# Order-only ties for the first chunk's gather, two places for the samples' states, expert rows from one queue, and an earlier fence slot

## Chip, cores and metric

The kernel runs on one core of a Trainium2 chip. The metric is the device time of one execution, in microseconds. The engines of the core are named as in the profile: PE (TensorE, matrix products; PEld is its weight load), DVE (VectorE), ACT (ScalarE), POOL (GpSimd) and SP (SyncE, which only issues transfers). Every engine works through its own list of instructions in the order in which they were placed at build time. ACT and SP issue plain transfers, each into a DMA queue of its own; POOL issues the indirect ones. All of them share 16 DMA engines.

## What is computed

One step of a decoder layer for 512 prompt tokens and 32 sample tokens (8 sequences of 4), model width 1024, all in float32:

```python
proj = x @ w_in + b_in                      # q, k, v, g, ca, cg: 512 columns each
q, k = rope(q), rope(k) * 128 ** -0.5
o, state = retention(q, k, v, state0)       # 4 heads, chunks of 128 tokens
ret  = silu(g) * head_norm(o)
conv = silu(layer_norm(depthwise31(ca * sigmoid(cg))))
x = layer_norm(ALPHA * x + concat(ret, conv) @ w_out)
# PEER: 8 heads, 128 x 128 product keys, the 16 best experts per head
idx, gate = topk(x @ w_query, sub_keys_1, sub_keys_2)     # 128 experts per token
act = gelu(u[idx] . x)
x = layer_norm(ALPHA * x + sum(gate * act * v[idx]))
```

There are 16384 experts, each with a row u and a row v of 1024 numbers. Besides the two y there go out the new retention states (one for the prompt, one for each sample sequence) and the new convolution caches.

## The kernel before, in words

The 544 tokens are laid out as the first prompt chunk (128 tokens), then the 32 samples, then the three other chunks. Two ways are used for the experts:

- **Gather.** For the first chunk, the samples and the second chunk, `gather` (L568 to L587) works slot by slot. A slot is one indirect transfer on POOL (L573) that fetches, for 128 (token, expert) pairs, u and v side by side, 8 KB each, into one buffer. DVE then takes the dot product of u with the token (L576, the "dot"), ACT applies gelu and the gate (L580, L581), and DVE adds v times the weight to the sum (L586, the "acc"). The first chunk has 128 slots, the samples 32 (four experts of each token at a time) and the second chunk 128. Four buffers go round for most of this (three in `gp`, one more in `gx` or `gx2`; three for the first chunk's slots from `KX` = 60 on).
- **Dense.** For the last 256 tokens, `scores_of` (L781) computes u of all 128 x 128 experts against the tokens on PE. A "key" is 128 experts: one row of 512 KB from the table `ut` (issued on L784), eight products on L787 (16 records in the profile), then gelu on ACT (L833, L838, or L886 and L888 in `s_stage`). The gates are put into a dense table by one-hot products (`build`, L858: ACT on L865 and L867, DVE on L869 and L873, PE on L878), and `first_keys` (L891) multiplies them into the scores (L902) or copies them (L904). Then `phases` runs over the rows of v, again 512 KB each (issued on L919), with products on L925 (8 records a row).

Rows of `ut` and `uv` go through four buffers (`UV`, L35), and `turns` (L774) issues them alternately from SP and from ACT.

The time runs in these stages. The first chunk goes through the whole layer up to its top-k first; then its gather slots are spread over the work on the other tokens: the samples' states (`retain_s`, L385), the convolution (L255) and its norm (`conv_norm`, L285), the retention of the three other chunks (`retain`, L704, with `head_norm`, L318), and the output projection with the layer norms (`mix_a` and `mix_b`, L723 to L738; `layer_norm`, L442; its transposes for the next product are on L487). Then come the query projection, the top-k of the other tokens (`retrieve`, L511) and, on PE, the scores of the first 76 keys. Then the build of `first_keys`, within which the scores of 20 more keys are made (`s_stage`). Its last product is the **fence**: the samples' slots from `FREE` = 24 on (L37, used on L577) and all slots of the second chunk have their dots behind it. Behind the fence `phases` (PE) and `fetched` (the rest of the gather, with `finish` and its stores on L596) run side by side. At the very end the last 256 tokens get their layer norm from PE's sums, and are stored.

`retain_s` goes over the eight sample sequences in pairs. Each round takes one tile from `keys_or_scratch` (a single buffer): its first half holds the states of two sequences (`r0`, loaded from ACT's queue on L404), the other half two copies of v, each masked to one sequence (`vx`, L403). PE uses the states (L408) and makes the update (L412, 256 columns), DVE adds it, and SP stores the new states (L415).

What orders the work: the tile framework simulates a timeline at build time, takes instructions in the order in which they can start there, and so fixes each engine's list. `behind(ins, other)` (L166) adds a tie that only says "not before this one in the list"; no semaphore is added by it. The fence is such a tie.

## Time and profile before

| quantity | value |
|---|---|
| median of 3 runs | 1601.7 us (1597.08 to 1602.1) |
| the profiled execution's own time | 1610.35 us |
| its span | 1608.6 us |
| mean granted clock of PE in it | 0.968 |
| DMA traffic | 503.75 MB, mean 313 GB/s |

The same page cuts the span into 40 slices of 40.2 us. A digit is the busy share of a slice in tenths; PEclk is the granted clock of PE, and 9 is 90% or more:

```profile
PE   6899989996879997999999997989999999999997
DVE  3939989989774999999866989667777677776642
ACT  2225352244221323333623799512994111111100
PEclk9999989997989999999999997999999999999999
DMA  9458678997789768998699721989999999999972
```

PE is the engine with the fullest row. The slices that are not full on PE lie at the start, at 200 us, at 360 to 480 us (the norms of the convolution and of the output projection), at 600 to 640, at 965 to 1005 us (the end of the build) and at 1045 to 1085 us. DVE follows the gather. ACT has its peak in the two builds (880 to 1000 us and around 1160 us). The DMA engines are nearly idle in the second half of the build and full from about 1085 us to 1530 us.

In the views quoted further down, a row of the waits tells which engine's operation waited, what for, the total in us, how often and the longest. A row of a timeline tells start and duration in us, engine, line, operation, output and inputs, and in square brackets the idle time before it with what ended it. A group of lines tells busy time, mean duration in ns of one, and the idle time before it.

### The profile page before, as it was taken

The numbers are of one execution on the slowest core, as the hardware profiler recorded it, in microseconds if no ns is written. First come the engines' busy times: TensorE is split into PE (matmuls) and PEld (weight loads), VectorE is DVE, ScalarE is ACT, GpSimd is POOL, SyncE is SP. The second block draws the span as 40 slices with busy tenths as digits, with TensorE's granted clock in tenths as the row PEclk, the third lists the DMA queues.
The fourth block names the chain that finished last, engine by engine and source line by source line (L and its number), as shares of the span: only waits on it lengthen the run. The fifth ranks groups of instructions, "written<-read, shape, count | busy, mean of one in ns | idle before, by whom it ended". The sixth has DMA issues, their size and how long they took to land.

```text
span 1608.6 us, 20726 instructions
## 1 busy us (share of the span) xinstructions
PE 1481.2 (92%) x7014; PEld 1016.0 (63%) x7014; DVE 1223.1 (76%) x3158; ACT 601.6 (37%) x1687; POOL 394.4 (25%) x335
## 2 busy tenths in 40 slices
PE   6899989996879997999999997989999999999997
PEld 6788557554666666888888885434566655644443
DVE  3939989989774999999866989667777677776642
ACT  2225352244221323333623799512994111111100
POOL 1001323433431222221122100233223223333200
PEclk9999989997989999999999997999999999999999
DMA  9458678997789768998699721989999999999972
GB/s 356 178 200 350 247 252 294 345 356 253 262 338 360 254 232 311 351 333 313 221 390 375 282 80 58 374 344 417 375 350 387 418 406 420 416 423 424 425 263 94
DMA packets 99542, 503.75 MB, mean 313 GB/s; under 512 B 10183, under 2 KB 21191, under 8 KB 56549
## 3 DMA queue, kind: packets, MB, share of 16 engines
q0 software_dynamic: 42240, 305.12, 48.9%
q1 hardware_dynamic: 32317, 122.84, 20.5%
q10 hardware_dynamic: 24880, 74.47, 12.4%
q8 instruction: 55, 0.90, 0.2%
q14 instruction: 50, 0.41, 0.1%
HBM read 497.03 MB, written 5.80 MB: 313 GB/s over the span
## 4 chain that ended last, share of the span: by engine, by line
PE 32%; DMA 28%; DVE 20%; issue 12%; POOL 5%; ACT 2%; ACTq 0%; POOLq 0%; SPq 0%; DVEq 0%
DMA g<-in_uv_dram,Ib 15%; PE pB L925 12%; PE sp L787 9%; DMA g<-in_uv_dram,I 8%; DVE acc L586 5%; PE mm L199 5%; POOL g L573 4%; DVE g L576 3%; PE mm L878 2%; DMA uv<-in_uv_dram 2%; DMA g<-in_w_in_dram 2%; DVE score L506 1%; PE mm L309 1%; PE mm L476 1%; DVE iu L505 1%
## 5 line engine op out<-in xcount | busy, mean ns | idle before, releaser
L787 PE MATMUL sp<-x1T,uv 128*128 128x256 f32 x2048 | 465.9, 383 | 25.4 <-DMA uv<-in_ut_dram 13.1
L787 PEld LDWEIGHTS sp<-x1T,uv 128*128 128x128 f32 x2048 | 386.0, 191 | 99.1 <-issue 27.7
L586 DVE SCALAR_TENSOR_TENSOR acc<-g,wgt,acc 128x1024 f32<-128x1024 f32 x285 | 364.8, 1280 | 102.1 <-ACT wgt L581 101.3
L573 POOL DMA_INDIRECT g<-in_uv_dram,I x128 | 177.1, 1384 | 451.9 <-DVE acc L586 253.5
L580 ACT ACTIVATE act<-act 128x1 f32<-128x1 f32 x288 | 57.8, 201 | 611.5 <-DVE g L576 599.9
L573 POOL DMA_INDIRECT g<-in_uv_dram,Ib x128 | 158.2, 1236 | 431.7 <-DVE acc L586 238.0
L576 DVE SCALAR_TENSOR_TENSOR g<-g,x1g 128x1024 f32<-128x1024 f32 x160 | 195.6, 1224 | 89.1 <-DMA g<-in_uv_dram,Ib 60.5
L576 DVE SCALAR_TENSOR_TENSOR g<-g,x 128x1024 f32<-128x1024 f32 x128 | 155.4, 1215 | 38.2 <-DMA g<-in_uv_dram,I 38.0
L199 PE MATMUL mm<-x1T,w 128*128 128x384 f32 (+1 forms) x512 | 177.6, 503 | 0.0
L925 PE MATMUL pB<-uv,Ga 128*128 128x512 f32 x352 | 157.2, 594 | 4.5 <-DMA uv<-in_uv_dram 4.4
L865 ACT ACTIVATE off<-row,e1T 128x128 bf16<-128x128 bf16 x512 | 157.7, 388 | 1.6 <-PE sp L787 0.6
L199 PEld LDWEIGHTS mm<-x1T,w 128*128 128x128 f32 x512 | 97.5, 192 | 71.9 <-issue 39.5
L925 PE MATMUL pB<-uv,Gb 128*128 128x512 f32 x256 | 117.4, 613 | 6.1 <-DMA uv<-in_uv_dram 5.6
L925 PEld LDWEIGHTS pB<-uv,Ga 128*128 128x128 f32 x352 | 66.3, 190 | 77.2 <-issue 67.4
L925 PE MATMUL pB<-uv,Gd 128*128 128x512 f32 x256 | 111.0, 593 | 2.9 <-DMA uv<-in_uv_dram 2.9
L925 PEld LDWEIGHTS pB<-uv,Gd 128*128 128x128 f32 x256 | 48.3, 190 | 65.4 <-issue 60.5
L925 PEld LDWEIGHTS pB<-uv,Gb 128*128 128x128 f32 x256 | 48.7, 196 | 64.2 <-issue 55.3
L878 PEld LDWEIGHTS <-A 128*128 128x128 bf16 x1536 | 64.4, 99 | 35.3 <-issue 26.3
L878 PE MATMUL mm<-B,A 128*128 128x96 bf16 (+1 forms) x1536 | 67.8, 196 | 11.6 <-DVE Gc L904 10.0
L873 DVE TENSOR_TENSOR B<-M,gtT 128x768 bf16<-128x768 bf16 (+1 forms) x192 | 69.5, 418 | 11.6 <-PE mm L878 11.6
L925 PE MATMUL pB<-uv,Gc 128*128 128x512 f32 x160 | 73.0, 601 | 0.0
L867 ACT ACTIVATE A<-off 128x1024 bf16<-128x1024 bf16 x64 | 67.4, 1053 | 14.4 <-PE mm L878 10.3
(279 smaller groups left out, 1701.5 us busy)
## 6 DMA issues: line engine op xcount, KB each, us to landing
uv<-in_ut_dram ACTq DMA_DIRECT2D x80, 512.0 KB
uv<-in_uv_dram SPq DMA_DIRECT2D x80, 512.0 KB
uv<-in_ut_dram SPq DMA_DIRECT2D x48, 512.0 KB
uv<-in_uv_dram ACTq DMA_DIRECT2D x48, 512.0 KB
w<-in_w_in_dram SPq DMA_DIRECT2D x18, 1024.0 KB
w<-in_w_query_dram SPq DMA_DIRECT2D x16, 1024.0 KB
w<-in_w_out_dram SPq DMA_DIRECT2D x7, 1024.0 KB
g<-in_uv_dram,I POOLq DMA_INDIRECT x128, 8.0
```

The source lines that it names most:

```text
L199: T.matmul(p[:, :n], w[m // 2][:, k, (m % 2) * 128:(m % 2 + 1) * 128], xT[:, k, c0:c0 + n], start=(k == 0), stop=(k == 7))
L309: mm = T.matmul(p[:n, q * 256:(q + 1) * 256], xT[:, k, c0:c0 + n], w[q][:, k, :], start=(k == 0), stop=(k == 7))
L573: G.indirect_dma_start(out=t, out_offset=None, in_=a["uv"], in_offset=bass.IndirectOffsetOnAxis(ap=idx[:, k:k + 1], axis=0))
L576: dot = V.scalar_tensor_tensor(t[:, :D], t[:, :D], 1.0, x1, op0=OP.mult, op1=OP.mult, accum_out=act[:, 0:1])
L580: S.activation(act[:, 1:2], act[:, 0:1], AF.Gelu)
L586: V.scalar_tensor_tensor(acc, v, wgt, acc, op0=OP.mult, op1=OP.add)
L787: T.matmul(sp, u[:, k], x1T[:, k, NG2:], start=(k == 0), stop=(k == 7))
L865: S.activation(off[:, t], row, AF.Abs, bias=e1T[:, t1 + t:t1 + t + 1])
L867: S.activation(A, off, AF.Relu, bias=1.0, scale=-1.0)
L873: V.tensor_tensor(B[:, q], M, pairs_of(gtT[:, q], t1).to_broadcast([128, TB // 2, ne, 2]), op=OP.mult)
L878: T.matmul(pt[:, t % nt], A[:, t - t1], B[:, q, (t - t1) // 2, :, t % 2], start=(q == 0), stop=(q == 2))
L925: T.matmul(pB[b][q], W[:, b * 128:(b + 1) * 128], vt[:, q * 512:(q + 1) * 512], start=False, stop=(e == NK - 1), skip_group_check=True)
```

## The change

Four things are changed.

1. `hold(k, ins)` notes that the first chunk's dots from slot k on stand behind `ins` on DVE. There are seven such notes: slot 48 behind the last small step of the second chunk's head norm, 50 behind the last multiplication of `conv_norm`, 52 behind the same head-norm step of the last chunk, and 56, 60, 64 and 68 behind the last addition of the four layer norms of `mix_b`.
2. `retain_s` takes one tile for all rounds. Its two halves hold the states of one pair and of the next in turn; the masked copies of v are two small tiles, and the update is two products of 128 columns in place of one of 256.
3. All rows of `ut` and `uv` are issued from SP. `turns` is gone.
4. `FREE` is 12 and no longer 24: the samples' slots from 12 on stand behind the fence.

```diff
--- before.py
+++ after.py
@@ -1,5 +1,4 @@
 from contextlib import ExitStack
-from itertools import cycle
 
 import numpy as np
 import concourse.bass as bass
@@ -34,7 +33,7 @@
 TB = 8
 KX = 60
 UV = 4
-FREE = 24
+FREE = 12
 EG = (32, 20, 44, 32)
 E0S = (0, 32, 52, 96)
 
@@ -297,10 +296,11 @@
         S.activation(rs[:, :n], pv[:, :n], AF.Sqrt, bias=eps_c)
         V.reciprocal(rs[:, :n], rs[:, :n])
         for m in range(4):
-            V.tensor_mul(y[:, m, :n], y[:, m, :n], rs[:, :n])
+            last = V.tensor_mul(y[:, m, :n], y[:, m, :n], rs[:, :n])
             S.activation(y[:, m, :n], y[:, m, :n], AF.Silu, bias=cg_b[:, m:m + 1], scale=cg_g[:, m:m + 1])
-
-    bv = [None]
+        return last
+
+    bv, steps = [None], {}
 
     def project_v(w, xT, c0, n, v=None, after=None):
         p = mmps()
@@ -327,7 +327,7 @@
         rsqrt(rs[:n], rs[:n])
         V.tensor_mul(rs[:n], rs[:n], cc("gq_" + kind)[:n])
         nb = small("hnb", [128, H])
-        V.scalar_tensor_tensor(nb[:n], mv[:n, :, 0], -1.0, rs[:n], op0=OP.mult, op1=OP.mult)
+        steps[kind] = V.scalar_tensor_tensor(nb[:n], mv[:n, :, 0], -1.0, rs[:n], op0=OP.mult, op1=OP.mult)
         on = small("on", [128, 512])
         for h in range(H):
             S.activation(on[:n, h * DH:(h + 1) * DH], po[:n, h * DH:(h + 1) * DH], AF.Identity,
@@ -395,12 +395,12 @@
         for h in range(H):
             T.matmul(po[:, h * n:(h + 1) * n], v[:n, h * DH:(h + 1) * DH], sc[:n, h * n:(h + 1) * n],
                      start=(h == 0), stop=False, skip_group_check=True)
+        room = keys_or_scratch()
         for b in range(0, SB, 2):
-            room = keys_or_scratch()
-            r0 = room[:, 0:D].rearrange("p (b h e) -> p b h e", b=2, h=H)
-            vx = room[:n, D:].rearrange("p (b e) -> p b e", b=2)
+            r0 = room[:, b // 2 % 2 * D:(b // 2 % 2 + 1) * D].rearrange("p (b h e) -> p b h e", b=2, h=H)
+            vx = [small("on", [128, 512]) for _ in range(2)]
             for j in range(2):
-                S.activation(vx[:, j], v[:n], AF.Copy, scale=cc("blk")[:n, b + j:b + j + 1])
+                S.activation(vx[j][:n], v[:n], AF.Copy, scale=cc("blk")[:n, b + j:b + j + 1])
             nc.scalar.dma_start(r0, a["state_retention"][0, b:b + 2].rearrange("b h d e -> d b h e"))
             for h in range(H):
                 for j in range(2):
@@ -409,7 +409,9 @@
                              start=False, stop=(h == H - 1 and b + j == SB - 1), skip_group_check=True)
             for h in range(H):
                 pk = mmps()[:, 0:256]
-                T.matmul(pk, kt[:n, h * DH:(h + 1) * DH], vx[:, :, h * DH:(h + 1) * DH], start=True, stop=True)
+                for j in range(2):
+                    T.matmul(pk[:, j * DH:(j + 1) * DH], kt[:n, h * DH:(h + 1) * DH], vx[j][:n, h * DH:(h + 1) * DH],
+                             start=True, stop=True)
                 V.scalar_tensor_tensor(r0[:, :, h], r0[:, :, h], float(GAMMA[h] ** SQ),
                                        pk.rearrange("p (b e) -> p b e", b=2), op0=OP.mult, op1=OP.add)
             nc.sync.dma_start(o[4][0, b:b + 2].rearrange("b h d e -> d b h e"), r0)
@@ -453,7 +455,7 @@
         for q, c in enumerate(halves if src else [slice(0, D)]):
             S.activation(t[:n, c], src[q][:n] if src else t[:n, c], AF.Identity, bias=rs[:n, 1:2], scale=rs[:n, 0:1])
             V.tensor_mul(t[:n, c], t[:n, c], g[:n, c])
-            V.tensor_add(t[:n, c], t[:n, c], b[:n, c])
+            steps["ln"] = V.tensor_add(t[:n, c], t[:n, c], b[:n, c])
 
     bv[0] = bc_row("b_v", a["b_in"][:, 1024:1536], 512, fe)
 
@@ -563,7 +565,11 @@
         V.reciprocal(sm[:n], sm[:n])
         V.tensor_mul(gate[:n, e0:e0 + nh], ex[:n], sm[:n].unsqueeze(2).to_broadcast([n, nh, TK]))
 
-    gx2, fence = [], []
+    gx2, fence, held = [], [], {}
+
+    def hold(k, ins):
+
+        held[k] = ins
 
     def gather(x1, idx, gate, acc, slots):
 
@@ -574,6 +580,10 @@
                                  in_offset=bass.IndirectOffsetOnAxis(ap=idx[:, k:k + 1], axis=0))
             act = gw.tile([128, 2], F32, name="act")
             dot = V.scalar_tensor_tensor(t[:, :D], t[:, :D], 1.0, x1, op0=OP.mult, op1=OP.mult, accum_out=act[:, 0:1])
+            if x1 is x1_0:
+                for k0, ins in held.items():
+                    if k >= k0:
+                        behind(dot, ins)
             if fence and (len(slots) == 128 or k >= FREE):
                 behind(dot, fence[0])
             wgt = gw.tile([128, 1], F32, name="wgt")
@@ -711,11 +721,12 @@
 
     retain(1)
     retain(2)
+    hold(48, steps["p"])
     banks[:] = [ps]
     silu_gate(wg, xT, n - NS, [(0, n - NS, gT[:, :, r])], False)
     wo = load_w(a["w_out"], 0) + load_w(a["w_out"], 512)
     S.activation(y[:, :, s_], yS, AF.Copy)
-    conv_norm(y, n)
+    hold(50, conv_norm(y, n))
     S.activation(gT[:, :, s_], gS, AF.Copy)
     banks[:] = [ps, ps, ps0, ps, ps0, ps, ps, ps0]
     xrs, pms, room = {}, {}, keys_or_scratch()
@@ -740,15 +751,20 @@
     gate_heads(ons[1], C, gT, NS)
     gate_heads(ons[2], C, gT, NS + C)
     retain(3)
+    hold(52, steps["p"])
     gate_heads(ons[3], C, gT, NS + 2 * C)
     mix_a(0, NS, None)
     mix_a(NS, C, 0)
     mix_b(0, NS)
+    hold(56, steps["ln"])
     mix_a(NS + C, C, 1)
     mix_b(NS, C)
+    hold(60, steps["ln"])
     mix_a(NS + 2 * C, C, None)
     mix_b(NS + C, C)
+    hold(64, steps["ln"])
     mix_b(NS + 2 * C, C)
+    hold(68, steps["ln"])
     caches()
     gather0 = gather(x1_0, I0, g0_gates, acc0, range(PH * TK))
     for _ in range(KX):
@@ -771,8 +787,6 @@
     ln2 = [bc_row("lng", a["ln2_g"], D), bc_row("lnb", a["ln2_b"], D)]
     GW = {2: gap.tile([128, EG[2], ND], F32, name="Ga")}
 
-    turns = cycle((nc.sync, nc.scalar))
-
     def place(e):
 
         g = max(i for i in range(4) if E0S[i] <= e)
@@ -781,7 +795,7 @@
     def scores_of(e):
 
         u = uvp.tile([128, D], F32, name="uv").rearrange("p (k e) -> p k e", k=8)
-        next(turns).dma_start(u, a["ut"][e])
+        nc.sync.dma_start(u, a["ut"][e])
         sp = pdn.tile([128, ND], F32, name="sp")
         for k in range(8):
             T.matmul(sp, u[:, k], x1T[:, k, NG2:], start=(k == 0), stop=(k == 7))
@@ -916,7 +930,7 @@
 
     def v_row(e):
         vt = uvp.tile([128, D], F32, name="uv")
-        next(turns).dma_start(vt, a["uv"][e * NK:(e + 1) * NK, D:])
+        nc.sync.dma_start(vt, a["uv"][e * NK:(e + 1) * NK, D:])
         return vt
 
     def v_products(e, vt, b):
```

## Prediction, made before the changed kernel had run

> **What bounds the kernel now.** I read the first part of the page, then the waits of TensorE, then the stretches in which those waits fall.
>
> ```profile
> span 1608.6 us, 20726 instructions
> PE 1481.2 (92%) x7014; PEld 1016.0 (63%) x7014; DVE 1223.1 (76%) x3158; ACT 601.6 (37%) x1687; POOL 394.4 (25%) x335
> ```
>
> ```profile
> PE mm L340 <- ACT on L333: 13.3, 2, 11.8
> PE sp L787 <- DMA uv<-in_ut_dram: 13.1, 12, 2.3
> PE pB L925 <- DMA uv<-in_uv_dram: 12.8, 10, 4.0
> ...
> PE mm L487 <- DVE xr L456: 10.5, 1, 10.5
> PE mm L878 <- DVE Gc L904: 10.0, 8, 2.2
> ...
> PE mm L487 <- DVE lrs L452: 5.9, 1, 5.9
> PE mm L408 <- DMA keys<-in_state_retention_dram: 4.9, 1, 4.9
> PE mm L412 <- ACT keys L403: 4.0, 1, 4.0
> ```
>
> TensorE is busy for 1481.2 of 1608.6 us, so 127.4 us are all that can be won without less matmul work or a better clock. The second view gives each wait as total, times and longest. The change aims at four groups of these lines: the sample states (4.9 + 4.0), the norms of mixing stage and convolution (11.8 + 5.9 + 10.5 = 28.2), the one-hot build (10.0), and the expert rows (13.1 + 12.8 = 25.9). Together that is 73 us. Three stretches show what else is busy there; the columns are sum of time, then PE, PEld, DVE, ACT and POOL busy, the granted clock, the DMA share and GB/s:
>
> ```profile
> 376.00:476.00 100.00, 74.03 (x369) 59.85 (x370) 79.32 (x126) 28.07 (x77) 39.64 (x32) 0.86 0.76 278
> 871.00:999.00 128.00, 116.60 (x1078) 100.16 (x1077) 117.16 (x404) 110.64 (x315) 8.25 (x8) 0.93 0.44 157
> 1284.00:1528.00 244.00, 228.72 (x675) 126.77 (x676) 170.57 (x216) 37.47 (x149) 75.07 (x66) 1.00 1.01 418
> ```
>
> In the mixing stage PE idles 26 of 100 us although nothing is full: a chain of short steps limits it. In the build three engines are at 86 to 92%. In the last one the DMA engines are full (418 GB/s) and PE loses 15.3 us. So there are three limits, and one edit for each.
>
> **Part 1, the sample states (L398 to L415).** Before, one tile holds two samples' states and the scaled copies of v, so the next load waits for the store of the last.
>
> ```profile
> 189.26 0.40 SPq L415 DMA_DIRECT2D out_dram<-keys  x1
> ```
> ```profile
> 200.75 0.38 ACTq L404 DMA_DIRECT2D keys<-in_state_retention_dram  x1
> ```
>
> The load at 200.75 came 11.5 us after the store was issued, and PE waited 4.0 us for the copies (L412 <- L403) and 4.9 for the states (L408): 8.9 us. After, the first two loads start together and the copies stand in tiles of their own, so both named waits should go. But the third load still needs the half that the first store reads, and it stands in PE's order with little between, so one such wait may come back later. The split product (two of 128 columns for one of 256) streams the same 256 columns in two instructions, and I take nothing for it. Bounds: 0 (the wait only moves to the third load) and −8.9. I take **−3**, nearer to 0, because the four loads are one after the other in the same stage and only one pair is taken apart.
>
> **Part 2, dots held behind norm steps.** VectorE's order is written at build time. Gather slots of the first chunk stand among the norms:
>
> ```profile
> L586 DVE SCALAR_TENSOR_TENSOR acc<-g,wgt,acc 128x1024 f32<-128x1024 f32 x24 | 30.6, 1277 | 2.0 <-ACT wgt L581 1.6
> L576 DVE SCALAR_TENSOR_TENSOR g<-g,x 128x1024 f32<-128x1024 f32 x23 | 27.9, 1218 | 13.3 <-DMA g<-in_uv_dram,I 13.3
> ```
> (VectorE, 376 to 476, grouped by line.) They take 58.5 of its 79.3 busy us, and in front of the dots it also idles 13.3 us for gather data, with norm steps queued behind the waiting dot. PE's gaps are the consequence; here is the last one, with its neighbours on VectorE:
>
> ```profile
> 475.02 1.09 PE L487 MATMUL mm<-cst,xr 128*128 128x128 f32 x4 [10.47 <-DVE xr L456]
> ```
> ```profile
> 467.72 0.16 DVE L452 SCALAR_TENSOR_TENSOR lrs<-lmv,lrs 128x1 f32<-128x1 f32 x1 [1.31 <-POOL lrs L185]
> 471.83 1.22 DVE L576 SCALAR_TENSOR_TENSOR g<-g,x 128x1024 f32<-128x1024 f32 x1 [3.95 <-DMA g<-in_uv_dram,I]
> ...
> 474.79 1.28 DVE L586 SCALAR_TENSOR_TENSOR acc<-g,wgt,acc 128x1024 f32<-128x1024 f32 x1
> ```
>
> In the last norm alone (from L452 to its last add), the wait of 3.95, the dot of 1.22 and the sum of 1.28 stand among its steps: 6.5 us. In the changed order, slots 68 on come after that norm (in the old order dots up to slot 73 stood ahead of its end), slots 56 to 67 after the three norms before it, and slots 48 and 50 after the two steps of the second chunk and of the convolution. That is five slots less ahead of the chain's end, 5 x (1.28 + 1.22) = 12.5 us, and the wait for data falls behind the norm. The chain is not VectorE alone (ScalarE, GpSimd and PE have steps in it), so not all of it comes off. I take **−11** for the instant at which L487 of the last chunk starts (475 to about 464). Bounds: −28.2 (the three waits gone) and +4 (there are four slot buffers: a dot held back holds back the transfers behind it on GpSimd's queue, and if the data then come late in front of a later dot, a wait like the 3.95 is added).
>
> The five slots are done later, and someone has to pay: the top-k of the other chunks shares VectorE with them:
>
> ```profile
> 640.00:800.00 160.00, 151.63 (x753) 131.28 (x754) 156.39 (x616) 65.93 (x160) 34.36 (x27) 0.99 0.84 305
> ```
>
> In the changed order the number of slots between the top-k's start and its first use by PE is unchanged, and the five extra ones come behind it, ahead of the end of top-k. PE has score keys to run there (L787), so I cost it at 0; if that cover fails it is 12.5 us of VectorE.
>
> **Part 3, the fence at slot 12.** The samples' slots 12 to 23 were done ahead of the fence (the build's last product into the table), and now stand behind it. Of these, the build held (VectorE, 871 to 999):
>
> ```profile
> L576 DVE SCALAR_TENSOR_TENSOR g<-g,x1g 128x1024 f32<-128x1024 f32 x8 | 9.7, 1218 | 0.0
> L586 DVE SCALAR_TENSOR_TENSOR acc<-g,wgt,acc 128x1024 f32<-128x1024 f32 x7 | 9.0, 1279 | 0.6 <-ACT wgt L581 0.6
> ```
> 18.7 of 117.2 us leave VectorE. But ScalarE is at 110.6 and PE at 116.6 of the 128, so VectorE at 98.5 stops being the bound and PE with its clock of 0.93 becomes it: 128 − 117 = **−11**. Bounds: −18.7 (the whole load) and −5 (half of the 10.0 us of waits L878 <- L904, which stand where all three are full).
>
> With −3, −11 and −11 the fence comes 25 us earlier:
>
> ```profile
> 998.67 0.23 DVE L902 TENSOR_TENSOR Gc<-Gc,mm 128x80 f32<-128x80 f32 x1
> ```
> ```profile
> L586 DVE SCALAR_TENSOR_TENSOR acc<-g,wgt,acc 128x1024 f32<-128x1024 f32 x128 | 164.4, 1284 | 68.4 <-ACT wgt L581 68.3
> ```
> ```profile
> 1545.54 1.29 DVE L593 SCALAR_TENSOR_TENSOR yt<-x1g,acc 128x512 f32<-128x512 f32 x2
> ...
> 1552.01 1.22 DVE L456 TENSOR_TENSOR yt<-yt,lnb 128x1024 f32<-128x1024 f32 x1
> 1594.22 0.70 DVE L448 BATCH_NORM_STATS2 lst<-pB 128x6 f32<-128x512 f32 x1 [40.99 <-PE pB L925]
> ...
> 1602.09 1.29 DVE L456 TENSOR_TENSOR g<-g,lnb 128x512 f32<-128x512 f32 x2
> ```
> ```profile
> 1531.29 65.47 PE L925 MATMUL pB<-uv,Gd 128*128 128x512 f32 x152 [0.86 <-DMA uv<-in_uv_dram]
> ```
>
> Behind the fence stood 8 + 128 slots and took 998.9 to 1545.5, 4.02 us each; now it is 148. From 974 that is 595 us, so the last sum ends at 1569 instead of 1545.5, its norm at 1577. PE's last product moves from 1596.8 to 1572. The 41 us in which VectorE waited are used up: both ends now meet, and the two final norms share VectorE (5.4 us of steps in the gather's one). I add **+4** (0 to +12).
>
> **Part 4, rows from one queue.**
>
> ```profile
> q0 software_dynamic: 42240, 305.12, 48.9%
> q1 hardware_dynamic: 32317, 122.84, 20.5%
> q10 hardware_dynamic: 24880, 74.47, 12.4%
> ```
> ```profile
> uv<-in_ut_dram ACTq DMA_DIRECT2D x80, 512.0 KB
> ...
> uv<-in_uv_dram ACTq DMA_DIRECT2D x48, 512.0 KB
> ```
> ```profile
> ACT act L580 <- DVE g L576: 599.9, 216, 7.9
> ```
> ```profile
> 1057.02 0.34 SPq L596 DMA_DIRECT2D out_dram<-yt  x1
> ```
> ```profile
> 1081.33 2.93 PE L925 MATMUL pB<-uv,Gb 128*128 128x512 f32 x3 [3.96 <-DMA uv<-in_uv_dram]
> ```
>
> 128 issues leave ScalarE, which stands waiting for dots for 599.9 us and issues late whatever is behind them. All 256 now leave SyncE, which has only stores to wait for; the samples' store at 1057.0 now comes after more rows, so the PE gap of 3.96 behind it should go or shrink. On the other side stands bandwidth. q0 moved 7.2 KB a packet, q1 3.8. In full stretches a row of 512 KB is needed about every 3.5 us (8 of the 152 products in 65.47 us: 3.45), which is 150 GB/s of 418. Nothing here shows one row queue alone for long beside a full gather. Bounds: −15.3 (all that PE lost from 1284 to 1528) and +18 (that loss, 6.3%, on all 598 us from fence to PE's last product is 37.5 us, of which 15.3 + 4.0 are lost already). I take **0**, as the rows that wait are mostly those that ScalarE issued late.
>
> The Trainium skill, page "DMA: Bandwidth & Descriptors", section "Queues, rings and completion order", says that each DMA engine goes round the queues that have work, packet by packet. By that rule one row queue gets one packet of two beside the gather where two got two of three; with the packets above that is 3.8 of 11.0 KB, 144 GB/s of 418 or 3.64 us a row, an estimate, 0.19 us over 3.45: +33 us on the 172 rows that the 595 us hold, if the gather never pauses, against the 0 taken above. No row of this trace tests it, since it never shows the two side by side for long.
>
> **Rivals.** (a) *The gather behind the fence becomes the end: slower.* Place: slots 12 to 31 of the samples and the 128 of the last chunk. Price: 12 x 4.02 = 48 us against 25 of fence and the slack of 41. With its norm and store (7.7 + 5.2 us) it ends at 974 + 148 s + 13. That is 1608.6 at s = 4.20 us a slot, 4% over today's; it is slower from there on. With s = 4.2 and a fence only 15 us earlier it ends at 1619, a time of 1612. For it: the DMA engines are full already, so 12 MB more have no free place. Against: PE's rows end with it, and when one lags the other's share is free. (b) *Row starvation.* The single row queue beside the full gather costs PE the 18 us of part 4's upper bound: −21 + 18, a time of 1599. For it: packets of 3.8 against 7.2 KB. Against: 15.3 us are lost already with two queues, half of them fed by an engine that issues late. The Trainium skill's rule quoted in part 4 is this mechanism. (c) *The holds give nothing.* The five slots come back under the top-k, where VectorE is busy for 156.4 of 160 us and has no place for 12.5 us more; if PE's score keys wait for it there, only states and build are won: −3 − 11 + 4 = −10, a time of 1592. For it: that row. Against: PE idles only 8.4 us there, with keys of its own to run. (d) *The change doesn't do what it says* in part 1: the third load waits as the second did. 3 us, inside the range.
>
> **How the numbers follow.** −3 − 11 − 11 + 0 + 4 = −21 on the profiled execution's span of 1608.6 gives 1587.6. The profiled execution's own time is 1610.35 us, 1.75 around its span and 8.65 above the median of the runs, 1601.7; the 21 come off that median: **1581** (1580.7). Chances: the forecast with (d) 0.52, (c) 0.14, (b) 0.16, (a) 0.18. Low end: part 2 at two thirds of its lower bound (18.8), the build likewise (12.5), the states at 3, the rows at 4, nothing at the tail: −38, so 1563. High end: beyond (b) and into the milder half of (a), 1606. About 0.3% (5 us) is what a measurement of this kernel can tell from no change: faster takes the forecast, (c) and 0.07 of (b), 0.73; the rest of (b) and 0.01 of (a) are 0.10; slower is 0.17.
>
> **What would show it.** Part 1: the two waits at L412 and L408 shorter, no 11 us between store and next load. Part 2: L340's 11.8 and L487's 10.5 down to a few us, L487's last start near 464, and no dot between L452 and L456 of that norm. Part 3: last L902 near 974, VectorE in the build below 100 us; the last sum near 1569 and the 41 us wait before the last norm gone. Part 4: PE's waits for rows at or under 26 us, and no wait near L596's store. I am wrong if the last L902 comes later than 990, if a slot behind the fence takes over 4.2 us, or if waits for rows exceed 45 us.

## The result, and the profile after

The changed kernel takes 1594.3 us (median of 20 runs, 1585.6 to 1603.8), the kernel before 1600.0 us (20 runs, 1594.8 to 1605.4, the three of above among them). The ratio is 0.9966, with a 95% interval of 0.9952 to 0.9981: by this ratio 5.4 us faster, where 21 were forecast. The profiled execution of the changed kernel took 1598.1 us. That is 12.2 us less than the profiled execution of before, which lies 10 us above its own median, so the two traces differ by more than the kernels do.

First part of its page, and its queues:

```profile
span 1595.8 us, 20861 instructions
PE 1499.0 (94%) x7046; PEld 1015.8 (64%) x7046; DVE 1225.1 (77%) x3158; ACT 602.9 (38%) x1686; POOL 365.0 (23%) x335
...
q1 hardware_dynamic: 50749, 189.96, 31.5%
q10 hardware_dynamic: 6448, 7.36, 1.5%
```

TensorE's waits (lines are those of the changed file: L487 is now L489, L476 is L478, L878 is L892, L787 is L801, L925 is L939):

```profile
PE mm L489 <- DVE xr L458: 13.1, 1, 13.1
PE mm L892 <- DVE Gc L918: 10.0, 8, 2.2
...
PE mm L478 <- ACT blk L300: 6.0, 1, 6.0
...
PE mm L408 <- DMA keys<-in_state_retention_dram: 3.2, 1, 3.2
PE pB L939 <- DMA uv<-in_uv_dram: 2.9, 4, 1.4
...
PE mm L340 <- ACT on L333: 1.6, 1, 1.6
...
PE sp L801 <- DMA uv<-in_ut_dram: 0.2, 1, 0.2
```

Most of the named waits shrank: 11.8 us at L340 are 1.6, the 5.9 in front of L487 are gone, 8.9 us for the states are 3.2, and 25.9 us for rows are 3.1. But the last norm's wait grew from 10.5 to 13.1, the build's 10.0 did not move, and 6.0 us appeared in front of the output projection (L478; e2, e4 and e6 have them too). Nor are the waits for rows gone. PE's own list leaves out its weight load, which waits for rows as well, before and after:

```profile
PEld pB L925 <- DMA uv<-in_uv_dram: 16.5, 10, 4.8
```
```profile
PEld pB L939 <- DMA uv<-in_uv_dram: 25.1, 46, 1.5
```

Few long waits have become many short ones. PE is also "busy" for 18 us more with almost the same products, and 10.6 of these stand in the products with rows of v (449.4 us before, 460.0 after). A record of such a product is 592 ns long, while the next one can start after 431 ns (152 in 65.47 us, before), so a pause of up to 0.16 us leaves no idle time in the records. The experiments show whose mark this is: e8, with one row queue, has 460.8 us in these products, and e2 and e13, with two, have 450.0 and 449.0.

This is the pace behind the fence, over the last 32 rows of v (256 records, 8 a row), before and after:

```profile
L925 PE MATMUL pB<-uv,Gd x256: 592/592/667, 1482.9 to 1596.2; 128*128 128x512 f32 x128
```
```profile
L939 PE MATMUL pB<-uv,Gd x256: 592/592/668, 1460.8 to 1579.4; 128*128 128x512 f32 x128
```

That is 3.54 us a row before and 3.71 after. The kernel before had the later half of these rows for itself, since its gather had ended at 1545: there a row took 3.43 us, and beside the gather 3.68. After, the gather runs to the end, and 3.7 us is also the step of its last slots (32 accs from 1460.2 to 1576.0). In the stretch from 1284 to 1528 the DMA engines move 424 GB/s, where it was 418:

```profile
376.00:476.00 100.00, 81.00 (x401) 62.51 (x400) 76.68 (x118) 30.91 (x80) 32.74 (x30) 0.90 0.70 267
1284.00:1528.00 244.00, 240.82 (x655) 118.62 (x654) 170.60 (x215) 38.98 (x148) 60.96 (x65) 1.00 1.02 424
```

### The profile page after: what moved, and what is told of

It reads as the page before. It is cut to its first block, busy times and chain, and to the rows that moved or that the text cites. A ratio compares the mean times of both kernels' runs of the same rounds, so it can differ in the third digit from the quotient of the medians.

```text
span 1595.8 us, 20861 instructions
## 1 busy us (share of the span) xinstructions
PE 1499.0 (94%) x7046; PEld 1015.8 (64%) x7046; DVE 1225.1 (77%) x3158; ACT 602.9 (38%) x1686; POOL 365.0 (23%) x335
## 4 chain that ended last, share of the span: by engine, by line
DMA 29%; PE 28%; DVE 24%; issue 9%; ACT 7%; POOL 3%; SPq 0%; DVEq 0%; POOLq 0%; ACTq 0%
DMA g<-in_uv_dram,Ib 18%; PE sp L801 9%; DMA g<-in_uv_dram,I 7%; DVE acc L596 6%; PE pB L939 5%; PE mm L198 4%; DVE g L582 4%; ACT off L879 3%; POOL g L579 2%; PE mm L478 2%; PE mm L263 2%; DMA g<-in_w_in_dram 2%; PE mm L892 2%; ACT A L881 1%; PE mm L309 1%
## 5 line engine op out<-in xcount | busy, mean ns | idle before, releaser
L801 PE MATMUL sp<-x1T,uv 128*128 128x256 f32 x2048 | 465.0, 384 | 14.2 <-ACT Ga L847 7.1
L596 DVE SCALAR_TENSOR_TENSOR acc<-g,wgt,acc 128x1024 f32<-128x1024 f32 x285 | 364.8, 1280 | 116.6 <-ACT wgt L591 113.8
L801 PEld LDWEIGHTS sp<-x1T,uv 128*128 128x128 f32 x2048 | 385.9, 192 | 87.4 <-issue 14.9
L579 POOL DMA_INDIRECT g<-in_uv_dram,I x128 | 164.9, 1288 | 468.0 <-DVE acc L596 236.0
L579 POOL DMA_INDIRECT g<-in_uv_dram,Ib x128 | 135.9, 1062 | 498.0 <-DVE acc L596 314.8
L939 PE MATMUL pB<-uv,Ga 128*128 128x512 f32 x352 | 162.1, 603 | 0.6 <-DMA uv<-in_uv_dram 0.4
L939 PE MATMUL pB<-uv,Gd 128*128 128x512 f32 x256 | 117.2, 601 | 2.1 <-DMA uv<-in_uv_dram 1.0
L939 PE MATMUL pB<-uv,Gb 128*128 128x512 f32 x256 | 115.4, 604 | 2.0 <-DMA uv<-in_uv_dram 1.4
L939 PEld LDWEIGHTS pB<-uv,Ga 128*128 128x128 f32 x352 | 63.7, 189 | 82.9 <-issue 63.1
L939 PEld LDWEIGHTS pB<-uv,Gd 128*128 128x128 f32 x256 | 46.1, 189 | 73.3 <-issue 71.5
L892 PEld LDWEIGHTS <-A 128*128 128x128 bf16 x1536 | 64.0, 99 | 34.7 <-issue 26.0
L939 PEld LDWEIGHTS pB<-uv,Gb 128*128 128x128 f32 x256 | 47.6, 192 | 58.8 <-issue 52.6
L892 PE MATMUL mm<-B,A 128*128 128x96 bf16 (+1 forms) x1536 | 67.7, 195 | 11.2 <-DVE Gc L918 10.0
L939 PE MATMUL pB<-uv,Gc 128*128 128x512 f32 x160 | 72.3, 599 | 0.0
```

The costliest lines, as they stand in the source:

```text
L579: G.indirect_dma_start(out=t, out_offset=None, in_=a["uv"], in_offset=bass.IndirectOffsetOnAxis(ap=idx[:, k:k + 1], axis=0))
L596: V.scalar_tensor_tensor(acc, v, wgt, acc, op0=OP.mult, op1=OP.add)
L801: T.matmul(sp, u[:, k], x1T[:, k, NG2:], start=(k == 0), stop=(k == 7))
L892: T.matmul(pt[:, t % nt], A[:, t - t1], B[:, q, (t - t1) // 2, :, t % 2], start=(q == 0), stop=(q == 2))
L939: T.matmul(pB[b][q], W[:, b * 128:(b + 1) * 128], vt[:, q * 512:(q + 1) * 512], start=False, stop=(e == NK - 1), skip_group_check=True)
```

## The experiments

Each kernel was timed beside the kernel before. The table has all of them, with three readings of the profiled execution: the start of the last norm's transposes (L487 or its like), the build (from the first to the last table product Gb), and the time from the fence to PE's last product. "Ties" are the seven order-only notes; a number there is the slot of the last one.

| kernel | states | ties | row queues | fence slot | last norm done | build | fence to PE's end | ratio to before (95%) |
|---|---|---|---|---|---|---|---|---|
| before | old | none | 2 | 24 | 475.0 | 127.8 | 598 | 1 |
| after | new | 68 | 1 | 12 | 466.9 | 127.9 | 594 | 0.9966 (0.9952 to 0.9981) |
| e1 | new | 68 | 1 | 24 | 465.3 | 133.9 | 597 | 1.0010 (0.9985 to 1.0035) |
| e2 | new | 68 | 2 | 12 | 467.7 | 126.1 | 595 | 1.0014 (0.9987 to 1.0041) |
| e3 | new | none | 1 | 12 | 481.5 | 126.0 | 592 | 1.0042 (1.0018 to 1.0066) |
| e4 | old | 68 | 1 | 12 | 457.2 | 126.0 | 594 | 0.9885 (0.9852 to 0.9918) |
| e5 | new | none | 2 | 24 | 475.4 | 126.1 | 598 | 1.0068 (1.0037 to 1.0099) |
| e6 | new | 66 | 1 | 12 | 463.4 | 126.0 | 592 | 0.9948 (0.9920 to 0.9975) |
| e7 | old | 68 | 1 | 20 | 456.2 | 126.5 | 597 | 0.9895 (0.9859 to 0.9932) |
| e8 | old | none | 1 | 24 | 461.5 | 126.0 | 600 | 0.9992 (0.9968 to 1.0015) |
| e9 | new, issue tied | 68 | 1 | 12 | 460.6 | 127.7 | 594 | 0.9916 (0.9889 to 0.9944) |
| e10 | old | 66 | 1 | 12 | 448.8 | 126.4 | 596 | 0.9868 (0.9841 to 0.9896) |
| e11 | old | 68 | 1 | 24 | 459.1 | 136.6 | 599 | 0.9973 (0.9951 to 0.9995) |
| e12 | old | 68 | 2 | 24 | 453.4 | 134.0 | 602 | 0.9984 (0.9960 to 1.0007) |
| e13 | old | none | 2 | 12 | 467.4 | 126.0 | 595 | 1.0022 (1.0001 to 1.0043) |
| e14 | new, issue tied | 66 | 1 | 12 | 450.3 | 126.0 | 594 | 0.9902 (0.9877 to 0.9927) |

One reading comes first. Up to their last norm, before, e8 and e13 have the same instructions in the same order on every engine (the first rows of `ut` apart, which e8 issues from the other queue), and that norm is done at 475.0, 461.5 and 467.4. So a single execution scatters by 13.5 us in this stage, and the one on which the prediction rests is the latest of the three (its time, 1610.4, stands 10 us above the median). The means over kernels with the same order up to that point are what can be compared: 468.0 (old states, no ties: before, e8, e13), 456.5 (old states, ties to 68: e4, e7, e11, e12), 478.5 (new states, no ties: e3, e5), 466.6 (new states, ties to 68: after, e1, e2). By them **the ties are worth 11.5 to 11.9 us, and the new states cost 10.1 to 10.5 us** at this place. Each mean has two to four executions, and the first one carries the whole scatter of 13.5, so the differences that use it are good to some 4 us. The timed runs, which don't rest on one execution, agree on the states: e5 is 0.7% (11 us) slower than before, and e4 0.8% (13 us) faster than the changed kernel.

The builds of 127.7 to 127.9 us (before, after, e9) differ from those of 126.0 in one thing that the profile shows: the mean granted clock from 50 to 60 us into the build is 0.83 there, and 1.00 in the others. Ten microseconds at 0.83 are 1.7 us of full clock.

**e1, the fence back at 24.** `-FREE = 12` `+FREE = 24`

> The changed kernel with the fence back at slot 24. Theory 1 (the build is not limited by VectorE: TensorE is full in its first two thirds, where the dots stood; behind the fence the DMA engines are the limit, a gather slot and a row going side by side at 3.70 us each): the build stays at 128 us although slots 12 to 23 stand in it again, the last acc comes 12 x 3.7 = 44 us earlier (about 1533), the last rows run at 3.45 us, PE's last product comes 5 to 7 us earlier and the tail shrinks from 15.8 to 12 us: about 10 us faster than the changed kernel, ratio to before 0.990. Theory 2 (the prediction: the build is limited by VectorE's 18.7 us of slots): build 139 us, tail 12: about 7 us slower than the changed kernel, ratio 1.001.

The build took 133.9 us, not 128, and the kernel is 0.4% slower than the changed one: theory 1 fell in its first half. Theory 2 has the ratio (1.001), but its build of 139 did not come either. The second half of theory 1 held: the last acc came at 1533.2, 44.1 us earlier, and the tail behind PE's end shrank from 15.8 to 11.7 us.

**e2, rows from two queues again.**

```diff
-        nc.sync.dma_start(u, a["ut"][e])
+        next(turns).dma_start(u, a["ut"][e])
```

> The changed kernel with rows issued alternately from SyncE and ScalarE again. Theory 1 (the sum of the bytes behind the fence is the limit, the queues only share it out): the row pace rises or falls against the slot pace, and the end moves by less than 4 us: ratio 0.994 to 0.999. Theory 2 (a single row queue gets one turn of two beside the gather and starves PE): rows faster than 3.70 us, slots slower than 3.75, PE's last product earlier by over 5 us. Theory 3 (rows issued late by ScalarE are the loss): PE's listed waits for rows back above 20 us, ratio above 1.000.

0.5% (8 us) slower than the changed kernel, and the trace shows only part of it: fence at 986.7 against 985.7, PE's end at 1581.9 against 1580.0, a tail of 18.4 us against 15.8. The longer tail is shared by e13, the other kernel with two queues and the fence at 12: in both the last acc comes 0.2 us or less before PE's end and the tail is 18.4; with one queue and this fence it comes 2.3 to 3.7 us before, and the tail is 14.9 to 16.0. The rows did not become faster with the second queue. The last 32 again take 3.7 us each:

```profile
L942 PE MATMUL pB<-uv,Gd x256: 592/592/668, 1464.2 to 1581.3; 128*128 128x512 f32 x128
```

So theory 2 fell. Theory 1 is right about the pace, but its ratio (up to 0.999) was missed. Theory 3 has only the ratio for it: PE's listed waits for rows are 17.7 us, under its 20.

**e3, no ties; e4, the old states.** For e3 `hold` notes nothing (`-held[k] = ins` `+return`); for e4 the loop of `retain_s` is that of before.

> The changed kernel without the seven ties of the first chunk's dots. Theory 1 (the ties are worth what the traces show between 362 and the start of L489 of the last chunk, 9 us, and it survives to the end): that start about 476 in place of 467, fence 994, ratio 0.9966 + 0.0056 = 1.002. Rival: what the ties win is given back under the top-k or behind the fence, where the DMA engines set the pace: ratio 0.996 to 0.998.

> The changed kernel with the samples' states in one place as before. Prediction: 3 us slower than the changed kernel, ratio 0.9985, with the waits of L412 and L408 at 4 and 5 us again. Rival (from the traces, 0.5 us between 150 and 360): the wait is only moved to other lines; same as the changed kernel within 2 us, ratio 0.995 to 0.998.

The ties held what was forecast of them: without them the last norm is done at 481.5 and the kernel is 0.8% slower. The states did the opposite: with the old ones it is 0.8% *faster*, although the waits at L412 and L408 are back (3.2 and 5.2 us). Neither theory on e4 had that.

**e5, the states alone; e6, the last tie at slot 66.** e5 is the kernel before with the new loop in `retain_s`; e6 is the changed kernel with `-hold(68, steps["ln"])` `+hold(66, steps["ln"])`.

> The kernel before with the edit of the samples' states alone. Theory S1 (two places remove the waits at L412 and L408 and cost nothing else): 0 to 4 us faster, ratio 0.9975 to 1.000. Theory S2 (the edit moves the gather's slots against the norms behind it, which costs more than the waits; in the changed kernel it was 11 us): 5 us or more slower, ratio 1.003 to 1.008, with the start of L487 of the last chunk later than 478 us. Theory S3 (the loss is a coincidence of this edit with the ties): 0.998 to 1.002 here, no loss without the ties.

> The changed kernel with the last tie at slot 66 in place of 68. In the changed kernel the dot of slot 66 waits 5.9 us for its data in front of the last layer norm's first step, and the dot of slot 67 stands behind its reciprocal. Theory H1 (a dot that waits for data ahead of a norm step holds up the norm; what is bound must be the dots whose data come late): the last start of L489 about 6 us earlier (461 in place of 467) and the whole 4 to 6 us faster than the changed kernel, ratio 0.993. Theory H2 (the order of the chain is set by PE, ScalarE and GpSimd): same as the changed kernel, 0.9966, within 2 us.

e5 bears out S2: 0.7% slower by this edit alone. Its last norm is done at 475.4, not later than 478 as S2 had it, but 7 us behind the mean of the kernels with the old order. For e6, these are VectorE's rows of the changed kernel around its last norm, for which PE had its sums ready at 453:

```profile
458.32 1.23 DVE L582 SCALAR_TENSOR_TENSOR g<-g,x 128x1024 f32<-128x1024 f32 x1 [5.93 <-DMA g<-in_uv_dram,I]
459.47 0.08 DVE L582 DVE_READ_ACCUMULATOR g<-g,x 128x1 f32 x1
459.47 0.69 DVE L450 BATCH_NORM_STATS2 lst<-mm 128x6 f32<-128x512 f32 x1
```

The dot of slot 66 stands ahead of the norm's first step (L450) and waits 5.93 us for data. In e6 it stands behind, and PE's wait there is 4.3 us in place of 13.1:

```profile
463.35 0.88 PE L489 MATMUL mm<-cst,xr 128*128 128x128 f32 x3 [4.29 <-DVE xr L458]
```

The mechanism H1 is shown, but the norm is done only 3 us earlier (463.4 against a mean of 466.6), and 3 us, inside the intervals, is all that the whole kernel gains (0.9948 against 0.9966): from there to the build it took 398 us against 391. With the old states (e10) the same tie won 8 us at the last norm, and 4 of them were left at the build.

**e7, old states and the fence at 20; e8, one queue alone.** e7 is e4 with `FREE = 20`; e8 is the kernel before with all rows from SyncE.

> The changed kernel with the samples' states as before (e4) and the fence at slot 20 in place of 12. Theory F1 (TensorE is full for the first 40 us of the build, so eight slots more fit there at no cost, and leave the stretch behind the fence): build 126 us as in e4, last acc 8 x 3.7 = 30 us earlier (about 1536), PE's last product 2 to 5 us earlier, tail 12 in place of 15: 5 to 8 us faster than e4, ratio 0.984 to 0.986. Theory F2 (every slot in the build costs VectorE time that is missed later in it): build 130 us or more, ratio 0.989 or above.

> The kernel before with the row queue edit alone: all rows from SyncE. Theory Q1 (prediction: nothing): ratio 0.998 to 1.002. Theory Q2 (from e2: the single queue saves 7 us, by ScalarE's late issues): 0.995 to 0.997, PE's listed waits for rows under 8 us. Theory Q3 (one turn of two beside the gather starves PE): rows at 3.70 us while the gather runs, 1.002 or above.

In e7 the build stays at 126.5 us with six dots in it, as F1 had it, and the last acc comes 30 us earlier, but the kernel is not faster than e4 (0.9895, where F1 had 0.984 to 0.986): from fence to PE's end it takes 597 us in place of 594. In all kernels with the fence at 20 or 24 this stretch takes 597 to 602, and with the fence at 12, which puts more slots behind it, 592 to 596; no run shows why. e8 changes nothing in the time that can be measured, as the prediction had it, although PE's listed waits for rows fall from 25.9 us to 3.5.

**e9, one issue tied behind a root.** What do the new states change 120 us later? These are the rows of the changed kernel around the convolution's norm, first GpSimd and then VectorE. The root of the head norm (L183, L184) and the gather's issues (L579) share GpSimd's list:

```profile
362.92 1.75 POOL L579 DMA_INDIRECT g<-in_uv_dram,I  x1 [3.85 <-DVE hrs L326]
364.70 1.13 POOL L183 TENSOR_SCALAR hrs<-hrs 128x4 f32<-128x4 f32 x1
365.91 1.05 POOL L184 TENSOR_TENSOR hrs<-hrs,mhalf 128x4 f32<-128x4 f32 x1
```
```profile
361.39 1.25 DVE L596 SCALAR_TENSOR_TENSOR acc<-g,wgt,acc 128x1024 f32<-128x1024 f32 x1
362.57 0.16 DVE L326 TENSOR_TENSOR hrs<-hmv,cst 128x4 f32<-128x4 f32 x1
...
367.00 0.16 DVE L328 TENSOR_TENSOR hrs<-hrs,cst 128x4 f32<-128x4 f32 x1 [1.25 <-POOL hrs L184]
367.08 1.08 DVE L291 TENSOR_TENSOR blk<-blk,mm 128x416 f32<-128x416 f32 x2
```

And with the old states (e4):

```profile
356.36 0.94 POOL L577 DMA_INDIRECT g<-in_uv_dram,I  x1 [1.46 <-DVE acc L594]
359.06 0.23 POOL L183 TENSOR_SCALAR hrs<-hrs 128x4 f32<-128x4 f32 x1 [1.75 <-DVE hrs L326]
359.37 1.05 POOL L184 TENSOR_TENSOR hrs<-hrs,mhalf 128x4 f32<-128x4 f32 x1
361.68 1.08 POOL L577 DMA_INDIRECT g<-in_uv_dram,I  x1 [1.26 <-DVE hnb L330]
```
```profile
354.83 1.27 DVE L594 SCALAR_TENSOR_TENSOR acc<-g,wgt,acc 128x1024 f32<-128x1024 f32 x1
```

GpSimd's list is the same here in both: 51 issues, slots 0 to 50, stand ahead of this root in every kernel but e9 and e14 (where it is 50). What the new states change is VectorE's list. Slot 50 goes into the buffer of slot 46, so its issue can start only when that slot's acc has ended. With the old states this acc ends 2.7 us before L326 starts, the issue is over when the root is needed, and the root starts 0.3 us after L326. With the new ones the same acc stands directly ahead of L326 in all eight kernels. The issue starts after it, the root waits behind the issue, and L328 runs 4.4 us after L326 instead of 2.5, with the convolution's subtractions (L291) behind it on VectorE. e9 ties the issue behind the root:

```diff
+    steps["pow1"] = steps["pow"]          # the root's last step, after retain(1)
...
+            if x1 is x1_0 and k >= 50:
+                behind(issue, steps["pow1"])
```

> The changed kernel, with the indirect transfers of the first chunk's slots from 50 on tied behind the power of the first chunk-norm's reciprocal root on GpSimd (order only). In the traces with the new states GpSimd's list has the issue of slot 50 (1.75 us, at 362.9) ahead of that root, and VectorE waits for it (L328) with the convolution's subtraction (L291) queued behind; with the old states the root stands ahead. Theory P1 (this order on GpSimd is what the new states cost): reciprocal of the convolution's norm 14 us after its mean's products in place of 19, and 4 to 6 us faster than the changed kernel, ratio 0.993. Theory P2 (the loss lies elsewhere, in the slots' place on VectorE): 17 us or more there, ratio 0.996 to 0.998.

The reciprocal of the convolution's norm comes 16.4 us after its mean's products, between the two theories (18.8 in the changed kernel, 14.2 in e4), and the kernel is 0.5% (8 us) faster than the changed one. L328 comes 2.55 us after L326 again. So the issue ahead of the root is a large part of what the new states cost. One statement of the expectation is wrong, though: with the old states the root does not stand ahead of slot 50's issue, which is merely over in time. And the share is not exact, since the tie also moves some instructions on the lists of the other engines.

**e10, old states and the tie at 66; e11, old states and the fence at 24; e12, the ties alone.**

> The changed kernel with the old states (e4) and the last tie at slot 66 (e6). Theory G1 (the two add up): last start of L487 at 451 in place of 457, ratio 0.985. Theory G2 (what the tie wins ahead of the top-k is lost under it, as in e6, where 398 us in place of 391 lay between the last norm and the build): last start at 451, but the build no earlier than 847, ratio 0.988 to 0.990.

> The changed kernel with the old states (e4) and the fence at slot 24 as before. Theory B1 (in e1 ten slots stood in the build, two of them past the first 40 us where TensorE is full, and stalled it once): if the build holds ten slots again it takes 131 to 134 us, ratio 0.992 to 0.994; if it holds eight, as before, 126 to 128, ratio 0.988 to 0.990. Prediction (VectorE limits the build, 11 us): build 137 us, ratio 0.995.

> The kernel before with the seven ties alone. Prediction: 11 us faster, ratio 0.993, last start of L487 11 us earlier than in the kernel before (461 to 475 in two executions, so 450 to 464). Rival: given back later, ratio 0.997 to 1.000, with the same earlier start.

e10 is the fastest kernel of all: 1580.4 us, 1.3% below before, between its two theories. e11 and e12 tell what the fence does. The ties alone bring the last norm to 453.4, yet the kernel wins nothing that is clear (0.9984, as the rival had it): its build takes 134.0 us, and the stretch behind it 602. With the fence at 12 the same order has 126.0 (e4), and the kernel is 0.9% faster than e11. e11's build of 136.6 is longer than its theory B1 had (131 to 134) and level with the prediction's 137, but a cost of VectorE time for every slot would also show with six or seven of them, and it doesn't. Where the dots stand in the build goes with it; the times are from its start:

| kernel | dots in the build | the last of them | build |
|---|---|---|---|
| e4, e13, after | 0 | | 126.0, 126.0, 127.9 |
| e5 | 6 | 29.5 | 126.1 |
| e7 | 6 | 25.4 | 126.5 |
| before, e8 | 7 | 31.2, 31.2 | 127.8, 126.0 |
| e1 | 9 | 46.0 | 133.9 |
| e12 | 10 | 47.6 | 134.0 |
| e11 | 10 | 49.3 | 136.6 |

Three stretches of 20 us of the build of before show why (columns as in the prediction):

```profile
871.00:891.00 20.00, 20.00 (x170) 17.77 (x169) 19.30 (x55) 13.81 (x44) 3.64 (x3) 1.00 0.86 322
891.00:911.00 20.00, 20.00 (x151) 17.71 (x151) 20.00 (x58) 15.05 (x45) 4.56 (x4) 1.00 0.88 302
...
971.00:991.00 20.00, 13.66 (x173) 10.43 (x172) 19.47 (x74) 19.71 (x54) 0.00 (x0) 0.82 0.08 28
```

In the first 40 us PE is full with the scores of the keys, and VectorE's seven slots stand beside it for nothing. From 971 on, where PE idles a third, VectorE and ScalarE are both nearly full without any slot. In e11 the dots reach into the third stretch, and PE loses 4 us of 20 there, where it lost 2 in the kernel before (17.96 busy from 911 to 931):

```profile
893.00:913.00 20.00, 16.02 (x139) 13.69 (x138) 19.72 (x62) 14.65 (x45) 2.81 (x3) 1.00 0.74 267
```

The loss of 8 to 11 us is more than the time of the one or two late slots (2.5 us each). In e1, e11 and e12 the granted clock is also lower from 40 to 70 us into the build (0.83 to 0.92 in one or two stretches of 10 us), which is at most 1.7 to 3.4 us of it; the rest is not taken apart.

**e13, the fence at 12 alone; e14, both repairs with the new states.**

> The kernel before with the fence at slot 12 alone. Theory K1 (eight slots in the build cost nothing there, since TensorE is full where they stand; the fence only pays where the ties have pushed ten or more slots into the build): build 126 to 128 us as before, twelve slots more behind the fence, both ends level: ratio 0.998 to 1.004. Prediction (VectorE limits the build): build 117 us, ratio 0.993 to 0.996.

> The changed kernel (new states) with both repairs: the issues from slot 50 on behind the reciprocal root on GpSimd (e9) and the last tie at slot 66 (e6). Theory W1 (the new states cost only by the order on GpSimd, and save a wait): level with the old states and the tie at 66 (0.9868) or better, 0.984 to 0.988. Theory W2 (the new states cost something else too): 0.989 to 0.992.

e13 settles the fence: alone it leaves the build where e8 has it (126.0) and makes the kernel a little slower (1.0022). e14 comes to 0.9902. That lies in W2's range, not in W1's, though its interval reaches into both and cannot be told from e10's (0.9868). With the issue tied, the new states are 0.3% behind the old ones in both pairs (e9 and e4, e14 and e10), each time inside the intervals. So a further cost of some 5 us is neither shown nor excluded, and nothing shows the new places to win.

## Why the prediction was wrong

The direction was right. The size was not: 5.4 us in place of 21. Point by point:

- **Part 1, the states: −3 forecast, +10 measured** at the last norm (by the means above) and +11 to +13 us in the time (e5, e4). This is the step that failed most. The two waits shrank from 8.9 to 3.2 us as described, but the step's bounds ended at 0 for the reason that "the wait only moves". The edit also moves the simulated timeline from which every later order is made. Among much else, 120 us later it set slot 46's acc back on VectorE's list, directly ahead of a step of a head norm; by that the issue of slot 50 came late, and the norm's root waited behind it on GpSimd. The changed order is a property of the kernel and needed no run; the prediction went through PE, VectorE and the row queues of the stage itself, and priced nothing for the lists behind it.
- **Part 2, the ties: −11 forecast, −11.5 to −11.9 measured** at the last norm. The number held, its working only in part. Slots 68 to 73 are six, not five, so 15 us of VectorE's time left the chain. And the wait for data did not fall behind the norm: it is the 5.93 us in front of the dot of slot 66, and slot 67's dot stands among the norm's steps. That the 475 us was the latest of three executions did not matter, since the difference was counted in slots and not in waits. What was wrong is that nothing is paid for it. The slots pushed back came into the build: ten dots where there were seven (e12).
- **Part 3, the build: −11 forecast, 0 measured against before** (127.8 to 127.9; 126.0 to 126.0 for e8 and e13). The step took one sum over 128 us, in which VectorE's 117.2 looked like the bound and PE's 116.6 like the length to which the build would shrink. Cut into stretches of 20 us, the same trace shows that the slots stood where PE was full. (One of the eight dots that were counted stands behind the fence.) The fence at 12 is worth 6 to 11 us of build, but only with the ties, which push dots past the first 40 us (e1 against after, e11 and e12 against e4). So it pays for part 2's bill rather than adding a gain.
- **Part 3, the tail: +4 forecast, +4.0 measured** (15.8 us from PE's last product to the end, where it was 11.8). The slots behind the fence took 4.00 us each (591.6 us for 148), as used; last acc at 1577 with a fence 11.7 us later than forecast.
- **Part 4, the rows: 0 forecast;** −0.8 per thousand alone (e8, no difference), −4.8 per thousand within the changed kernel (e2). The price of 0 stands for the kernel before; why the second queue costs 8 us in the changed one stays open, but for the 2.6 us of tail.
- **The rivals.** (b), the starved rows, was right in the pace: a row takes 3.71 us beside the gather, 141 GB/s, where the rule of the Trainium skill (page "DMA: Bandwidth & Descriptors", section "Queues, rings and completion order") gave an estimate of 3.64. But e2 has 3.7 us with two queues, and the kernel before had 3.68 beside its gather, so the pace is not that of the single queue, and the estimate's nearness is luck. What they have in common is the full DMA traffic, 418 to 424 GB/s from 1284 to 1528. (a) had s = 4.00, below its point of 4.20. (c) was half right: the ties' gain was given back, not under the top-k but in the build, where the fence saved it.
- **The signs.** Of the three signs of being wrong none came: the last table product at 985.7 (not later than 990), slots of 4.00 us (not over 4.2), listed waits for rows of 3.1 us (not over 45). The first was set too wide to tell: with the ties' 11 us alone the fence lies at 988.

Taken together: −11.5 from the ties, +10 from the states, 0 in the build, 0 to −8 from the rows, about 4 won between fence and PE's end and +4 of tail, which is between −1.5 and −9.5; 5.4 were measured. The single sizes come from different kernels and do not add up exactly; the fence and the ties are worth more together than apart.

Not settled: what makes up the rest of what the new states cost before e9's tie. Some of it lies ahead of 360 us. From 300 to 350 PE is busy for 44.0 to 48.9 us in the eight kernels with the new states, and for all 50 in seven of the eight with the old ones (46.8 in before). In the changed kernel it waits there for ScalarE, in e4 it doesn't:

```profile
306.43 1.65 PE L208 MATMUL mm<-blk,cst 128*128 128x384 f32 x2 [2.43 <-ACT blk L218]
```

Nor was the edit of the states taken apart. Besides the two places it splits a product, and it takes the masked copies of v from the same two buffers (`on`) into which the head norm writes; no run says which of the three moves the orders.

## What to carry to other kernels

Before a stage is priced by an engine's busy sum, cut it into stretches short enough that the bound doesn't change within one; work that stands where another engine is full cost nothing here, and taking it away won nothing. Where orders are made by a simulated timeline, an edit has a second price in every list behind it: compare them all, and together, since a step's place on one engine sets when an instruction on another can start. Look for a long issue ahead of a short step that someone waits for, and for what that issue waits for. And one profile is one draw: here identical orders differed by 13.5 us in one stage, two and a half times the whole effect.

## What the hardware showed that I had not expected

A TensorE that is hardly ever listed as waiting can still be held up. Beside a full gather a row of eight products took 3.7 us with one row queue and with two, in place of 3.43. With two queues the waits are long enough to be listed (12.8 us on PE for rows of v, in 10 pieces). With one they are 46 short ones on the weight load, and the products' records, longer than the step between them, cover them up: 460 us "busy" for the same products in place of 449. And GpSimd's issue of an indirect transfer (0.9 to 1.8 us each in the rows above) holds up every short step behind it: 1.75 us of issue ahead of a root put 1.9 us more between two steps of a norm (4.4 us, and 2.55 in e9), and the tie that takes it away made the whole kernel 8 us faster.
